# One key page group of sixteen turned by VectorE instead of TensorE, in a hybrid decoder layer

## The chip, the cores and the metric

The kernel runs on one core of a Trainium2 chip. The metric is device time in microseconds of one execution, as the median of several runs; the profile is of one execution. The engines are named as in the profile: PE (TensorE matmuls), PEld (its weight loads), DVE (VectorE), ACT (ScalarE), POOL (GpSimd) and SP (SyncE, which issues most of the transfers).

## The reference: one layer of differential attention, a gated delta rule and a conv-FFN

One decoder layer runs over a prompt of 512 tokens with 16 learned meta tokens ahead of it, and over 8 sample sequences of 8 new tokens, each with 2048 past tokens in a paged cache of 128 tokens a page. The change lies in the attention of the sample sequences:

```python
def diff_attn_sample(q, k, v, lam, k_past, v_past):
    qs = q * (d ** -0.5)
    s_past = jnp.einsum('bqhmd,bkhmd->bhmqk', qs, k_past)
    s_new = jnp.einsum('bqhmd,bkhmd->bhmqk', qs, k)
    s_new = jnp.where(jnp.tril(...), s_new, -jnp.inf)
    pr = jax.nn.softmax(jnp.concatenate([s_past, s_new], axis=-1), axis=-1)
    a = pr[:, :, 0] - lam * pr[:, :, 1]
    ...
k_past = cache_k[l][page_table].reshape(ds, -1, DA_HEADS, 2, DA_HEAD_DIM)
```

There are 4 heads with two maps of 64 channels each, so a key has 512 channels, and a page of keys is 128 x 512 floats, 256 KB. The same layer has the prompt's own differential attention (`o_a`, with an RMS norm over each head), the gated delta rule in chunks (`o_b`), one combined input projection, two sigmoid gates, an output projection and a gated FFN with a causal convolution of width 3.

## The kernel before

Everything is fp32. A product of fp32 operands is made from three products of high and low parts (`xhi`, `xlo`, `whi`, `wlo`): weights arrive as `wraw` (line 430), ACT casts the high part (line 434), DVE subtracts the low part (line 435). All matmuls are issued by `mm` (line 381) and all TensorE transposes by `transpose` (line 541).

Two generators run interleaved. `main()` does the projections, the prompt's attention head by head (`prompt_attention`) and the delta rule; `rest()` does the sample sequences' attention (`sample_attention`), the gates and branch products. `merge` counts PE work as it is issued (`self.work`) and resumes the generator that is furthest behind; a generator that has yielded a number stays away for so much PE work. The numbers come from the table `PAUSES`, by generator and index of the yield, else from the code. `Held` marks a pause that also holds while narrow work runs, and a planner then settles the order on each engine. Each engine runs its own instructions strictly in that order.

**The sample attention.** For each of four pairs of sequences (`pr`) and each of four key groups (`g`), eight pages are loaded, two pages a tile `page` (six buffers). SP issues the loads (line 1575) with an address read from the page table. Keys arrive with tokens on the partitions; the score matmul needs channels there. So PE turns each page by four transposes of 128x128 into `ps_t`, ACT or DVE copies the result to `KT` (line 1596), and 16 matmuls make the scores `ps_s<-KT,qb`. A DVE instruction (`score`, line 1427) adds the mask and takes the maximum.

**The prompt attention of one head.** For blocks of rows, the scores `ps_m` go through `score`, ACT's exponential and normalising on DVE (lines 1505 to 1512) to `S`; PE turns `S`, ACT or DVE copies it to `aT`, and `ps_t<-v,aT` and `ps_t<-vt,aT` give the output block, which ACT copies to `on` (line 1529). After the last block `head_norm` runs: four squares with sums on ACT (`hjunk`, line 1538), a multiply-add on DVE (`hss`, line 503), a power on POOL (line 504), and four scalings on DVE (`on`, line 1541). Then PE turns `on`.

The group concerned (`pr` 0, `g` 2) is issued while the first head of the prompt's attention is at its last blocks.

Of the kernel before, what the change touches and what calls it, by code (L numbers as in the profile page):

```python
# [24 lines left out]
NPG = PAST // PAGE  # L25
H = 4
# [25 lines left out]
def _lay_out_constants():  # L52
# [67 lines left out]
    for name, a in (("c0", c0), ("c1", c1), ("m0", m0), ("m1", m1)):  # L120
# [27 lines left out]
PAGES = 6  # L148
CUT_S = 832
CUT_O = 512  # L150
MAKE_W = 54.400005891
WRAW, WLO = 3, 4
LOADS_AHEAD = 5
NC = 290
# [4 lines left out]
WARM = 5  # L159
FINE = 8  # L160
MAIN_1 = 564.54
HOLD = 3.0
PAUSES = {
# [4 lines left out]
    },  # L168
# [4 lines left out]
    },  # L173
# [5 lines left out]
    },  # L179
# [4 lines left out]
    },  # L184
    "gdn_project0": {
        0: 0.24, 4: 0.94, 6: 4.89,
# [2 lines left out]
        2: 0.06, 3: 1.09, 4: 0.27, 6: 11.27,  # L189
    },  # L190
    "gdn_project2": {
        0: 0.09, 2: 0, 3: 1.19, 5: 0, 6: 9.74,
    },
# [5 lines left out]
    },  # L199
    "make0": {  # L200
        5: 1.23, 6: 0.56, 7: 0.9, 10: 0.5, 13: 0.26, 16: 0.4,
    },
    "prompt_rows0": {
        0: 6.89, 1: 1.2, 3: 7.45, 4: 0.72,
    },
    "prompt_rows1": {
        0: 2.75, 1: 0.86, 4: 1.45,
    },
    "prompt_rows2": {
        0: 7.54, 1: 1.83, 3: 7.27, 4: 1.59, 5: 0.86,  # L210
    },
    "prompt_rows3": {
        0: 7.41, 1: 1.54, 2: 0.01, 3: 2.6, 4: 0.98,
    },
    "prompt_rows4": {
        1: 1.26, 3: 3.04, 4: 2.18,
    },
    "prompt_rows5": {
        2: 0.03, 4: 0.59,
    },  # L220
    "prompt_rows6": {
        0: 7.63, 1: 1.37, 3: 1.06, 4: 1.41,
    },
    "prompt_rows7": {
        1: 1.2, 3: 2.57, 4: 1.29,
    },
# [12 lines left out]
    },  # L239
    "use0": {  # L240
        0: 0.07, 5: 1.68, 6: 0.1, 9: 0, 12: 6.56, 13: 0.11, 23: 0.6, 25: 10.39, 26: 0.26, 38: 2.47, 39: 0.1,
        51: 3.07,
    },
}
MAIN_2 = 1e9
# [11 lines left out]
class Body:  # L257
# [40 lines left out]
    def run(self):  # L298
        nc, ctx = self.nc, self.ctx
# [13 lines left out]
        with ExitStack() as sm:  # L313
            with ExitStack() as s1:
                self.opool = self.pool(s1, "opool")
                self.oa = self.t(self.opool, [128, H, NQ], "oa")
                self.ob = self.t(self.opool, [128, H, NQ], "ob")
                with ExitStack() as s2:
                    self.keep = self.pool(s2, "keep")
                    self.x = self.parts(self.pool(s2, "xpool"), "x", 8, HALF_T)  # L320
                    with ExitStack() as s:
                        first = self.embed(self.pool(s, "embed", 2, side="right"))
                    self.gproj = self.pool(s2, "gproj")
                    da = ExitStack()
                    dpool = self.pool(da, "da")
                    self.psum_m = self.pool(da, "psum_m", space=PSUM)
                    self.da_queries(dpool, first)
                    with ExitStack() as s:
                        tmp = self.pool(s, "gs", side="right")
                        self.gdn_scalars(tmp)  # L330
                        self.gdn_consts(tmp)
                    self.news = self.chain = self.spare = False

                    swo, self.wo0, self.wo_next = ExitStack(), [], 0

                    def main():
                        head = {}
                        yield from self.da_main(dpool, self.gdn_project(0, head))
                        da.close()
                        self.chain = True  # L340
                        self.psum_g = self.pool(ctx, "psum_g", space=PSUM)
                        with ExitStack() as s:
                            self.gpool = self.pool(s, "gpool")
                            yield from self.gdn(head)
                        yield from self.mix_parts(self.pool(s2, "mix"))
                        self.wo0 += self.wout_tiles(self.pool(swo, "wo0", side="right"), 0)

                    def rest():
                        with ExitStack() as s:
                            yield from self.sample_attention(self.pool(s, "sa", side="right"))  # L350
                        self.gates, self.gtpool = {}, self.pool(sm, "gates", side="right")
                        for i in range(16):
                            yield from self.gate(i)
                        while not self.spare:
                            yield None
                        yield from self.branch_a()

                    self.drain(self.merge((main(), lambda: MAIN_2 if self.chain else MAIN_1), (rest(), REST_W)))
                    self.banks = "ggsttdd"
                    self.mix()  # L360
# [1184 lines left out]
    def sample_attention(self, pool):  # L1545
        nc, a = self.nc, self.a
# [4 lines left out]
        ck = a["cache_k"][0].rearrange("n t h m d -> n t (h m d)")  # L1551
# [18 lines left out]
        def pages(cache, ids):  # L1570
# [5 lines left out]
                moves[tag] = move.ins  # L1576
            return t

        for pr in range(NB // 2):
            if pr % 2 == 0:  # L1580
                os = self.t(pool, [128, 1, 128], "oS", bufs=1)
# [1 line left out]
            mx = self.t(self.keep, [128, 5], "smx", bufs=2)  # L1583
            for g in range(4):
                sp = self.ps("s")
                kts = {}
                for u in range(2):
                    for e in range(2):
                        kp = pages(ck, [(2 * pr + e) * NPG + 4 * g + 2 * u + j for j in range(2)])
                        kt = self.t(pool, [128, H, 256], "KT", bufs=4)  # L1590
# [8 lines left out]
                for u in (1, 0):  # L1599
                    for e in (1, 0):  # L1600
                        for h in range(H):
                            self.mm(
                                sp[32 * h : 32 * h + 32, 256 * u : 256 * u + 256], self.qb[:, 2 * pr + e, h],
                                kts[u, e][:, h], start=e == 1, stop=e == 0,
                            )
                yield 0.0
# [852 lines left out]
```

## Time and profile before

| | |
|---|---|
| median of 3 runs | 1110.27 us (1109.65 to 1110.64) |
| the profiled execution | 1109.7 us, its span 1107.9 us |
| PE / DVE / ACT / POOL busy | 98% / 66% / 47% / 20% |
| page transposes on PE (line 541) | 512, 69.3 us busy |
| copies to `KT` on ACT (line 1596) | 108, 58.6 us busy |
| score matmuls `ps_s<-KT,qb` | 512 records, 34.1 us busy |

The profile gives each group of instructions as line, engine, operation, output<-input by the program's names, shape, count, busy time and mean duration. In a timeline or a chain row the first number is the start in us, the second the time. A row of a table of windows has the window, its length, then the busy time (and count) of PE, PEld, DVE, ACT and POOL, the granted clock, the share of the DMA engines, and GB/s. Matmuls overlap, so from one start to the next is less than the duration of one.

### The profile page before, as it was taken

The numbers are of one execution on the slowest core, as the hardware profiler recorded it, in microseconds if no ns is written. First come the engines' busy times: TensorE is split into PE (matmuls) and PEld (weight loads), VectorE is DVE, ScalarE is ACT, GpSimd is POOL, SyncE is SP. The second block draws the span as 40 slices with busy tenths as digits, with TensorE's granted clock in tenths as the row PEclk, the third lists the DMA queues.
The fourth block names the chain that finished last, engine by engine and source line by source line (L and its number), as shares of the span: only waits on it lengthen the run. The fifth ranks groups of instructions, "written<-read, shape, count | busy, mean of one in ns | idle before, by whom it ended". The sixth has DMA issues, their size and how long they took to land.

```text
span 1107.9 us, 23301 instructions
## 1 busy us (share of the span) xinstructions
PE 1082.5 (98%) x8554; PEld 958.0 (86%) x8554; DVE 726.1 (66%) x1891; ACT 521.2 (47%) x1258; POOL 220.4 (20%) x340
## 2 busy tenths in 40 slices
PE   8999999999999999999999999999999999999997
PEld 7888887787786787799999978999999999988886
DVE  6456667686468586465335754699999999842315
ACT  6335454465464465344333344465565555832311
POOL 4122230211101110100000004335454444200000
PEclk9999999999999999999999999999999999999999
DMA  6395325747956767722234263323233332333213
GB/s 198 78 326 164 99 72 186 255 150 250 311 189 213 237 209 229 234 69 66 72 95 135 86 180 124 115 67 107 87 98 96 96 98 77 120 111 105 90 44 124
DMA packets 167356, 156.88 MB, mean 142 GB/s; under 512 B 12307, under 2 KB 123458, under 8 KB 167241
## 3 DMA queue, kind: packets, MB, share of 16 engines
q1 hardware_dynamic: 162833, 147.00, 43.2%
q0 software_dynamic: 3008, 5.16, 1.5%
q10 hardware_dynamic: 1400, 3.22, 0.9%
q8 instruction: 68, 1.11, 0.4%
q14 instruction: 47, 0.39, 0.1%
HBM read 145.45 MB, written 9.88 MB: 140 GB/s over the span
## 4 chain that ended last, share of the span: by engine, by line
PE 80%; DVE 8%; ACT 4%; DMA 3%; issue 3%; POOL 2%; SPq 0%; DVEq 0%; ACTq 0%; POOLq 0%
PE ps_d L381 30%; PE ps_t L381 21%; PE ps_g L381 15%; PE ps_s L381 6%; PE ps_t L541 6%; ACT KT L1596 1%; PE ps_m L381 1%; DMA wraw<-in_w_out 1%; DVE wlo L435 1%; DVE cy L880 1%; DMA x<-in_x_prompt 1%; DMA page<-in_cache_v 1%; DVE xc L1217 1%; DVE row L1215 1%; DVE row L1216 1%
## 5 line engine op out<-in xcount | busy, mean ns | idle before, releaser
L435 DVE TENSOR_TENSOR wlo<-wraw,whi 128x512 fp32r<-128x512 f32 x190 | 143.2, 771 | 112.3 <-ACT whi L434 111.5
L381 PE MATMUL ps_d<-xhi,whi 128*128 128x256 f32 (+2 forms) x696 | 213.0, 309 | 0.2
L381 PE MATMUL ps_d<-xlo,whi 128*128 128x256 f32 (+2 forms) x696 | 209.6, 304 | 0.0
L381 PE MATMUL ps_d<-xhi,wlo 128*128 128x256 f32 (+2 forms) x696 | 209.1, 303 | 0.0
L434 ACT CAST whi<-wraw 128x512 fp32r<-128x512 f32 x190 | 114.0, 620 | 155.5 <-PE ps_d L381 62.2
L381 PEld LDWEIGHTS ps_d<-xlo,whi 128*128 128x128 f32 x696 | 130.7, 189 | 4.5 <-issue 4.2
L381 PEld LDWEIGHTS ps_d<-xhi,whi 128*128 128x128 f32 x696 | 130.8, 189 | 4.3 <-issue 2.6
L381 PEld LDWEIGHTS ps_d<-xhi,wlo 128*128 128x128 f32 x696 | 130.7, 189 | 1.7 <-issue 1.2
L1596 ACT COPY KT<-ps_t 128x512 f32<-128x512 f32 x108 | 58.6, 601 | 34.5 <-PE ps_t L541 28.5
L435 DVE TENSOR_TENSOR lw<-sw,hw 128x512 fp32r<-128x512 f32 x76 | 69.7, 918 | 5.2 <-ACT hw L434 5.2
L541 PE MATMUL ps_t<-consts,page 128*128 128x128 f32 x512 | 69.3, 278 | 2.5 <-DVE KT L1596 1.1
L381 PE MATMUL ps_t<-fhit,hw 128*128 128x290 f32 x228 | 67.9, 298 | 0.5 <-DVE p L2124 0.5
L381 PE MATMUL ps_t<-flot,hw 128*128 128x290 f32 x228 | 67.6, 296 | 0.0
L381 PE MATMUL ps_t<-fhit,lw 128*128 128x290 f32 x228 | 67.5, 296 | 0.0
L541 PEld LDWEIGHTS ps_t<-consts,page 128*128 128x128 f32 x512 | 56.2, 140 | 10.1 <-issue 2.7
L434 ACT CAST hw<-sw 128x512 fp32r<-128x512 f32 x76 | 46.8, 618 | 15.7 <-PE ps_g L381 10.5
L381 PEld LDWEIGHTS ps_t<-fhit,hw 128*128 128x128 f32 x228 | 43.1, 189 | 0.9 <-DVE p L2124 0.7
L2099 ACT ACTIVATE fy<-fpre,fw 128x592 f32<-128x592 f32 x22 | 19.4, 884 | 50.8 <-DVE fpre L2059 50.8
L381 PEld LDWEIGHTS ps_t<-flot,hw 128*128 128x128 f32 x228 | 43.2, 189 | 0.0
L381 PEld LDWEIGHTS ps_t<-fhit,lw 128*128 128x128 f32 x228 | 43.0, 189 | 0.0
L2101 DVE SCALAR_TENSOR_TENSOR fy<-fpre,fw,fy 128x592 f32<-128x592 f32 x44 | 36.4, 828 | 1.0 <-ACT fy L2099 0.4
L381 PE MATMUL ps_s<-KT,qb 128*32 128x256 f32 x512 | 34.1, 383 | 1.5 <-ACT KT L1596 1.2
(722 smaller groups left out, 2805.1 us busy)
## 6 DMA issues: line engine op xcount, KB each, us to landing
page<-in_cache_k SPq DMA_DIRECT2D x128, 256.0 KB, 4.5
page<-in_cache_v SPq DMA_DIRECT2D x128, 256.0 KB, 4.0
wraw<-in_w_in SPq DMA_DIRECT2D x86, 256.0 KB, 3.2
wraw<-in_w_ffn_in SPq DMA_DIRECT2D x50, 256.0 KB, 3.0
wraw<-in_w_down SPq DMA_DIRECT2D x44, 256.0 KB, 3.0
raw<-in_w_ffn_in SPq DMA_DIRECT2D x38, 256.0 KB, 2.9
wraw<-in_w_out SPq DMA_DIRECT2D x16, 256.0 KB, 3.0
x<-in_x_prompt SPq DMA_DIRECT2D x4, 512.0 KB, 7.4
```

What stands on the lines that cost most here:

```text
L381: i = self.nc.tensor.matmul(out, lhsT, rhs, **kw)
L434: self.nc.scalar.copy(hi, raw)
L435: (eng or self.nc.vector).tensor_tensor(out=lo, in0=raw, in1=hi.bitcast(F32), op=ALU.subtract)
L541: i = self.nc.tensor.transpose(out, in_, self.ident[:k, :k])
L880: nc.vector.scalar_tensor_tensor(out=y, in0=pre[:, j : j + n], scalar=self.cw[:, ch, 24 + j : 25 + j], in1=y, op0=ALU.mult, op1=ALU.add)
L1215: nc.vector.stream_shuffle(r, y, [i // BASE * BASE + j for i in range(32)])
L1216: nc.vector.tensor_tensor(out=r, in0=r, in1=lc[:, :, j : j + 1].to_broadcast([128, 5, j + 1]), op=ALU.mult)
L1217: nc.vector.tensor_tensor(out=y, in0=y, in1=r, op=ALU.subtract)
L1596: copy(kt[:, :, 128 * j : 128 * j + 128], tp)
L2099: nc.scalar.activation(y, pre[:, 0:592], AF.Identity, bias=fw[:, m, 19:20], scale=fw[:, m, 16:17])
L2101: nc.vector.scalar_tensor_tensor(out=y, in0=pre[:, j : j + 592], scalar=fw[:, m, 16 + j : 17 + j], in1=y, op0=ALU.mult, op1=ALU.add)
```

## The change

For one group of the sixteen (`TURNED`), the eight pages are loaded by 32 DMAs of 64 KB instead of 8 of 256 KB. Each moves, for one page, one 32-channel block out of every 128 channels to one quarter of the partitions, in runs of 128 bytes; the token index is split so that partition p of a quarter holds every fourth token. DVE then turns all 32x32 blocks of a tile in place, one instruction of 128x1024 for two pages, and the tile holds channels on the partitions. The 16 score matmuls read the tile itself, and write their output with strides (`keys`), so that the tokens come out in order. The 32 PE transposes and the 8 copies to `KT` (six on ACT, two on DVE) of that group are gone. Besides, `main()` waits for the end of `sample_attention` before `mix_parts`, and nearly all entries of `PAUSES` and one weight of the merge (`MAKE_W`) have new values. Lines behind the new code move by 6 and more: 541 is 547, 381 is 387, 1541 is 1547.

```diff
-MAKE_W = 54.400005891
+MAKE_W = 65.82400712811001
+L_P = 4.0
+T_P = 4.0
+TURNED = ((2,), (), (), ())
...
     "rest0": {
-        0: 0.35, 1: 1.56, 2: 0.55, 4: 0.71, 6: 0.07, 8: 1.04, 10: 1.68, 12: 1.45, 13: 1.35, 14: 1.02, 16: 4.8,
+        0: 0.35, 1: 1.56, 2: 0.55, 4: 0.71, 10: 1.66, 12: 1.45, 13: 1.35, 14: 1.02, 16: 4.8, 17: 1.03, 21: 1.11,
...
+                        while not self.sampled:
+                            yield None
                         yield from self.mix_parts(self.pool(s2, "mix"))
...
                             yield from self.sample_attention(self.pool(s, "sa", side="right"))
+                        self.sampled = True
...
+        def blocks(ids):
+
+            t = self.t(pool, [128, 2, 512], "page", bufs=PAGES)
+            for k, i in enumerate(ids):
+                tag, value = entry(ck, i)
+                page = cache_blocks[bass.ds(value, 1)]
+                for c in range(4):
+                    move = nc.sync.dma_start(
+                        t[32 * c : 32 * c + 32, k].rearrange("p (n d) -> p n d", d=32),
+                        page[:, :, :, c].rearrange("o t n d -> (o t) n d"),
+                    )
+                moves[tag] = move.ins
+            return t
+
+        cache_blocks = ck.rearrange("n (t b) e -> n t (b e)", b=4).rearrange("n t (m c d) -> n t m c d", c=4, d=32)
...
-                kts = {}
-                for u in range(2):
+                kts, keys = {}, lambda x: x
+                for u, e in [(u, e) for u in range(2) for e in range(2)] if g in TURNED[pr] else []:
+                    kts[u, e] = blocks([(2 * pr + e) * NPG + 4 * g + 2 * u + j for j in range(2)])
+                if kts:
+                    yield L_P
+                    for kp in kts.values():
+                        two = kp.rearrange("p j c -> p (j c)")
+                        nc.vector.transpose(two, two)
+                    kts = {a: kp.rearrange("p j (b h t) -> p h j b t", b=4, h=H) for a, kp in kts.items()}
+                    keys = lambda x: x.rearrange("p (j t b) -> p j b t", t=32, b=4)
+                    yield Held(T_P)
+                for u in range(0 if kts else 2):
...
-                                sp[32 * h : 32 * h + 32, 256 * u : 256 * u + 256], self.qb[:, 2 * pr + e, h],
+                                keys(sp[32 * h : 32 * h + 32, 256 * u : 256 * u + 256]), self.qb[:, 2 * pr + e, h],
```

The order on PE around the group's scores `ps_s_1363`, at the end of the first head. Before, from the last output block of the head (`ps_t_1486`) on:

```order
L381 MATMUL ps_t_1486<-v_954,aT_1478 128x128 [waits Activation_49]
L381 MATMUL ps_t_1486<-vt_358,aT_1478 128x128 [waits DVE_49]
L381 MATMUL ps_s_1363<-KT_1447,qb_356 32x256 x4
L381 MATMUL ps_s_1363<-KT_1431,qb_356 32x256 x4
L381 MATMUL ps_s_1363<-KT_1401,qb_356 32x256 x4
L381 MATMUL ps_s_1363<-KT_1376,qb_356 32x256 x4
L541 MATMUL ps_t_1533<-consts_66,page_1520 128x128 [waits DMAHW6_49,PE_49]
L541 MATMUL ps_t_1533<-consts_66,page_1520 128x128 x3
```

Now, from the same output block (`ps_t_1462`) on; `page_1364`, `page_1382`, `page_1400` and `page_1409` are the group's four tiles in the order in which DVE turns them:

```order
L387 MATMUL ps_t_1462<-v_954,aT_1454 128x128 [waits Activation_49]
L387 MATMUL ps_t_1462<-vt_358,aT_1454 128x128 [waits DVE_49]
L387 MATMUL ps_s_1363<-page_1409,qb_356 32x2x4x32 [waits DMAHW4_49,DMAHW3_49,DMAHW5_49,DMAHW2_49,DMAHW6_49,DMAHW1_49,DMAHW7_49,DMAHW0_49,DVE_49]
L387 MATMUL ps_s_1363<-page_1409,qb_356 32x2x4x32 x3
L387 MATMUL ps_s_1363<-page_1400,qb_356 32x2x4x32 x4
L387 MATMUL ps_s_1363<-page_1382,qb_356 32x2x4x32 x4
L387 MATMUL ps_s_1363<-page_1364,qb_356 32x2x4x32 x4
L547 MATMUL ps_t_1509<-consts_66,page_1496 128x128 [waits DMAHW6_49,PE_49]
```

The place of the scores is the same; they now wait for DVE, at the tile turned last. Between the head's last `ps_m` and this place stood 32 page transposes and 18 product matmuls before; none stands there now. On DVE before, at the same place (`S_736` is the score instruction of the group, `hss` and `on` belong to head_norm):

```order
L1523 COPY aT_1478<-ps_t_1482 16x128
L503 TENSOR_SCALAR hss_1490<-hss_1490 128x4
L1427 ISA S_736,smx_737<-ps_s_1363,consts_66 128x512
L1427 ISA smx_737 128x1
L1541 SCALAR_TENSOR_TENSOR on_1098<-on_1098,hss_1490,sub_562 128x128 x4
L1596 COPY KT_1532<-ps_t_1533 128x4x128
```

and now (the turn of `page_1364` stands 37 instructions ahead of this `hss`):

```order
L1529 COPY aT_1454<-ps_t_1458 16x128 [waits PE_49,Pool_49]
L509 TENSOR_SCALAR hss_1466<-hss_1466 128x4 [waits Activation_49]
L1547 SCALAR_TENSOR_TENSOR on_1098<-on_1098,hss_1466,sub_562 128x128 [waits Pool_49]
L1614 STREAM_TRANSPOSE page_1382<-page_1382 128x1024 [waits DMAHW4_49,DMAHW5_49,DMAHW3_49,DMAHW6_49,DMAHW2_49,DMAHW7_49,DMAHW1_49,DMAHW0_49]
L1547 SCALAR_TENSOR_TENSOR on_1098<-on_1098,hss_1466,sub_562 128x128 x3
L1614 STREAM_TRANSPOSE page_1400<-page_1400 128x1024 [waits DMAHW4_49,DMAHW5_49,DMAHW3_49,DMAHW6_49,DMAHW2_49,DMAHW7_49,DMAHW1_49,DMAHW0_49]
L1614 STREAM_TRANSPOSE page_1409<-page_1409 128x1024 [waits DMAHW4_49,DMAHW5_49,DMAHW3_49,DMAHW6_49,DMAHW2_49,DMAHW7_49,DMAHW1_49,DMAHW0_49]
L1433 ISA S_736,smx_737<-ps_s_1363,consts_66 128x512 [waits PE_49]
```

Three turns stand behind `hss` and the first `on`, and the score instruction, which stood between `hss` and `on`, has moved behind the turns. On SP, the group's 32 loads stand where its 8 stood; the loads of the next two tiles and of the weights (`wraw`) follow them as before.

More of the change, by code (lines that the diff above doesn't have):

```diff
@@ L191 @@
     "gdn_project2": {
-        0: 0.09, 2: 0, 3: 1.19, 5: 0, 6: 9.74,
+        0: 0.02, 2: 0, 3: 0.54, 5: 0, 6: 9.74,
     },
     "main0": {
[4 rows of a table removed]
[4 rows of a table added]
     },
     "make0": {
-        5: 1.23, 6: 0.56, 7: 0.9, 10: 0.5, 13: 0.26, 16: 0.4,
+        1: 0.36, 4: 0.16, 5: 2.42, 6: 0.6, 7: 0.9, 10: 0.5, 13: 0.26, 16: 0.4,
     },
     "prompt_rows0": {
-        0: 6.89, 1: 1.2, 3: 7.45, 4: 0.72,
+        0: 2.06, 1: 1.2, 3: 7.45, 4: 0.46,
     },
     "prompt_rows1": {
-        0: 2.75, 1: 0.86, 4: 1.45,
+        0: 2.75, 1: 0.86, 3: 4.52, 4: 1.45,
     },
     "prompt_rows2": {
-        0: 7.54, 1: 1.83, 3: 7.27, 4: 1.59, 5: 0.86,
+        0: 7.54, 1: 1.83, 3: 7.43, 4: 1.86, 5: 0.86,
     },
     "prompt_rows3": {
-        0: 7.41, 1: 1.54, 2: 0.01, 3: 2.6, 4: 0.98,
+        0: 6.65, 1: 0.92, 2: 0.01, 3: 2.6, 4: 0.28,
     },
     "prompt_rows4": {
-        1: 1.26, 3: 3.04, 4: 2.18,
+        1: 0.67, 3: 3.04, 4: 2.17,
     },
     "prompt_rows5": {
-        2: 0.03, 4: 0.59,
+        1: 0.75, 2: 0.01, 4: 0.59,
     },
     "prompt_rows6": {
-        0: 7.63, 1: 1.37, 3: 1.06, 4: 1.41,
+        0: 7.72, 1: 1.37, 3: 1.06, 4: 1.41,
     },
     "prompt_rows7": {
-        1: 1.2, 3: 2.57, 4: 1.29,
+        1: 1.2, 3: 2.5, 4: 1.29,
     },
     "rest0": {
[11 rows of a table removed]
[11 rows of a table added]
     },
     "use0": {
-        0: 0.07, 5: 1.68, 6: 0.1, 9: 0, 12: 6.56, 13: 0.11, 23: 0.6, 25: 10.39, 26: 0.26, 38: 2.47, 39: 0.1,
-        51: 3.07,
+        0: 0.05, 5: 1.16, 6: 0.1, 9: 0, 12: 5.34, 13: 0.11, 19: 0, 23: 0.24, 25: 13.34, 26: 0.26, 27: 0.54,
+        38: 2.47, 39: 0.1, 51: 3.07,
     },
@@ L331, in run @@
                         self.gdn_consts(tmp)
-                    self.news = self.chain = self.spare = False
+                    self.news = self.chain = self.spare = self.sampled = False
                     swo, self.wo0, self.wo_next = ExitStack(), [], 0
```

52 rows, old and new, of the table PAUSES are left out of this document.

## The prediction

> **What bounds the kernel now.** I read the page's busy shares first, then PE by stage, then the chain of waits around the place where the turned group will stand.
>
> ```profile
> span 1107.9 us, 23301 instructions
> PE 1082.5 (98%) x8554; PEld 958.0 (86%) x8554; DVE 726.1 (66%) x1891; ACT 521.2 (47%) x1258; POOL 220.4 (20%) x340
> L541 PE MATMUL ps_t<-consts,page 128*128 128x128 f32 x512 | 69.3, 278 | 2.5 <-DVE KT L1596 1.1
> 60.00:112.00 52.00, 51.42 (x442) 43.04 (x440) 32.85 (x108) 24.53 (x62) 13.20 (x25) 1.00 0.75 250
> 112.00:560.00 448.00, 434.66 (x4213) 363.66 (x4213) 290.08 (x1013) 223.68 (x630) 55.43 (x106) 1.00 0.57 176
> ```
>
> PE is busy for 98% of the span, and the time is in first order PE's work plus the gaps in it. So whatever leaves PE is gained in full, and whatever makes PE wait is lost in full, DVE's, ACT's and the DMA's own work counting only where PE stands behind it. From 60 to 112 us, where the turned group lies, PE is idle for 0.58 us; from 112 to 560 us for 448 − 434.66 = 13.3 us.
>
> **What is taken from PE.** 32 of the 512 page transposes go.
>
> ```profile
> 95.17 0.45 PE ps_m L381 x4
> ...
> 99.34 0.24 PE ps_d L381 x2
> 99.58 1.55 PE ps_t L541 x14
> ...
> 103.60 0.69 PE ps_t L381 x4
> 104.28 0.02 issue
> 104.31 0.28 ACT on L1529
> ...
> 104.61 0.41 ACT hjunk L1538 x2
> ...
> 106.60 1.06 POOL hss L504
> ...
> 107.69 1.14 DVE on L1541 x4
> ```
>
> These are pieces of the chain of waits. Fourteen transposes take 1.55 us of it, 0.111 us each, so 32 give **−3.5 us**. The eight copies to KT that leave ACT and DVE hide behind PE today; what they free is counted at nothing. The 16 score matmuls stay. Their output is now strided in PSUM; no row has that form, so it costs between 0 and once more their present time (1.93 us, the 104.20 row below). I take 0, because it is the same number of elements from the same kind of matmul.
>
> **What PE waits for now.** In the order of PE, the head's last two matmuls with aT (ps_t<-v,aT and ps_t<-vt,aT) are followed directly by the turned scores, and the first of these reads the page that VectorE turns last. On VectorE the last three turns stand behind head_norm: after hss and the first `on`. head_norm itself starts from those same two matmuls. In the chain above, the matmuls end at 104.28 us; ACT's copy, four squares with their sums, DVE's hss and POOL's power come next, and the first `on` starts at 107.69, 3.41 us later. Before, PE had score matmuls, page transposes and products to do in that time:
>
> ```profile
> 103.89 0.39 PE L381 MATMUL ps_t<-vt,aT 128*128 128x128 f32 x2
> 104.20 1.93 PE L381 MATMUL ps_s<-KT,qb 128*32 128x256 f32 x32
> 106.07 1.53 PE L541 MATMUL ps_t<-consts,page 128*128 128x128 f32 x12
> 109.48 2.10 PE L541 MATMUL ps_t<-consts,page 128*128 128x128 f32 x16 [0.52 <-DVE KT L1596]
> L1225 DVE STREAM_TRANSPOSE cc<-row x4: 338/346/346, 265.4 to 508.4; 128x160 f32<-128x160 f32 x4
> L1261 DVE STREAM_TRANSPOSE row<-cc x4: 306/311/313, 268.9 to 513.6; 128x128 f32<-128x128 f32 x4
> ```
>
> After, it has nothing: everything later in its order stands behind the scores. Their release needs 3.41 us, four `on` (1.14 us) and three turns of 128x1024. The two nearest rows give 311 ns at 128 columns and 346 at 160, 1.09 ns a column, so 1024 columns take 311 + 896 x 1.09 = 1.29 us, or 1.25 us from one to the next with some overlap. The gap is 3.41 + 1.14 + 3 x 1.25 = **+8.3 us**. If a turn went at half the time a column the gap would be 6.4, if at twice 12.0. I take the slope, since both rows are the same instruction on the same type. The first turn stands 37 instructions ahead of hss and adds 1.2 us to a VectorE that is 63% busy (32.85 of 52 us): nothing.
>
> **What the lost filler uncovers.** The 32 page transposes and 18 product matmuls that stood between the head's last ps_m (ends 95.62) and its last ps_t<-vt,aT (ends 104.28) also covered the softmax between them. Without them, PE has 104.28 − 95.62 − 3.55 − 2.1 = 3.0 us to do there (18 products at 0.12, from the pair at 99.34). The chain that it waits for is on VectorE and ACT:
>
> ```profile
> 97.01 0.34 DVE L1427 CUSTOM_DVE_ANT_0 S<-ps_m,consts,mx 128x128 f32<-128x128 f32 x1
> 98.41 0.67 DVE L1389 COPY v<-ps_t 128x512 f32<-128x512 f32 x1
> 99.23 0.41 ACT L1503 ACTIVATE S<-S,nm 128x144 f32<-128x144 f32 x1 [0.61 <-DVE nm L1501]
> 102.31 0.37 DVE L1512 SCALAR_TENSOR_TENSOR S<-S,rc,S 128x144 f32<-128x144 f32 x1
> 103.34 0.28 DVE L1523 COPY aT<-ps_t 16x128 f32<-16x128 f32 x1 [0.66 <-PE ps_t L541]
> ```
>
> Two maps' scores and maxima come to about 1.4 us (the 128-wide one 0.34, its neighbours 0.1 to 0.2), the copies of v and vt that stand between them 0.9, the exponential with its sum 0.6, normalising 0.8, then PE's two transposes 0.4, the copy 0.28 and the last matmuls 0.66: 5.0 us against 3.0. Exposed: **+1.9 us** (0.5 if VectorE's copies of v come earlier, 2.5 at most). VectorE's copies of KT stood in this chain too and go, which I have left out of the sum of 5.0 already. The stall of 0.52 us at 109.48, on a copy of VectorE's, is overtaken by the longer one: **−0.5**.
>
> **PE after a long gap.** The span's first matmuls are the only ones that follow a long idle time; the last two rows are PE's longest single waits from 112 to 560 us (total, times, longest).
>
> ```profile
> 1.10 2.50 PE L381 MATMUL ps_s<-warm 128*128 128x128 f32 x10 [1.10 <-DVE warm L556]
> 3.39 2.59 PE L381 MATMUL lnb<-row,one 128*128 128x512 f32 x4
> 5.82 0.38 PE L381 MATMUL ps_s<-warm 128*128 128x128 f32 x2
> PE ps_s L381 <- DMA page<-in_cache_v: 1.7, 2, 1.3
> PE ps_t L541 <- DVE on L1541: 1.2, 1, 1.2
> ```
>
> The same matmul takes 0.21 to 0.23 us from start to start at 1.1 us ((2.50 − 0.42) / 9, where 0.42 is one alone) and 0.11 at 5.8 us (0.38 − 0.27). So PE runs at half pace there for between 2.3 and 4.7 us, though the clock column reads 1.00 from the first slice on. No single wait of those is longer than 1.3 us, so whether 8 us bring the slow start back isn't seen. If they do, PE loses half of 2.3 to 4.7 us, 1.2 to 2.4. I take **+1.5**, because part of it falls on page transposes that wait for their copies anyway; if they don't, 0.
>
> [...]
>
> **The transfers.** Eight loads of 256 KB become 32 of 64 KB in runs of 128 bytes.
>
> ```profile
> 66.26 10.00 SPq L1575 DMA_DIRECT2D page<-in_cache_k  x12
> 76.55 15.06 SPq L430 DMA_DIRECT2D wraw<-in_w_in  x4
> L1575 SPq DMA_DIRECT2D page<-in_cache_k x128: 332/333/1207, 55.3 to 417.6; - x128
> q1 hardware_dynamic: 1492, 0.12, 19.4%
> 80.00:88.00 8.00, 7.94 (x57) 7.29 (x58) 5.61 (x23) 3.23 (x9) 1.76 (x5) 1.00 0.29 76
> ```
>
> SP spends 0.33 us on one issue and, with the queues full of 256-KB loads, 10.00 / 12 = 0.83 us from one to the next, so 32 take 11 to 27 us from 66.26. On the 16 DMA engines, the queue row (of the window from 16 to 24 us: 1492 packets of 80 bytes on average) gives 0.194 x 8 us x 16 / 1492 = 17 ns a packet; 16384 packets make 17 us. From 80 us on the engines are 71% free. I expect the last to land at about 90 us; the last three turns run from 108. So this is hidden: each load would have to take (107.7 − 66.3) / 32 = 1.29 us before the last turn were late. Behind the 32 on SP stand four loads of wraw and the next pages. With 24 issues more ahead of them, at 0.33 to 0.83, wraw leaves 8 to 20 us later than 76.55; its products stand behind the turned scores, after 112, so it is hidden too, with less room.
>
> **The rest.** The table of pauses is retuned throughout and moves products from this stage to later ones. The wait for the sample attention before mix_parts costs nothing (the last keys are loaded at 417.6 us, the row of L1575, and the delta rule, which main has to end first, still turns blocks at 508.4 us, the row of L1225). I take 0 for the retuning, between −6 and +2: the gain can come from the 13.3 us of idle PE alone.
>
> **Sum**: −3.5 + 8.3 + 1.9 − 0.5 + 1.5 = +7.7 on the profiled execution's 1109.7 us, 1117.4. The median of the runs is 0.57 above that execution, so **1118.0 us**.
>
> **Rivals.**
> 1. *The gap stays, the slow start doesn't come*: 1116.5. For it: the clock column never leaves 1.00. Against: the first matmuls.
> 2. *Faster: the slack is given back.* In the gap ACT, VectorE and the queues run ahead, and the later waits of PE (13.3 us in 112 to 560) shrink. Against rival 1's 1116.5 it decides from 6.2 us given back on, and with 8.5 the time is 1108.0. For it: the waits are on ACT, VectorE and loads, all of which could be early. Against: the next head's own head_norm, the last row of the fence on the long gap, is a chain that starts from PE itself, so a head start doesn't shorten it. Between 4 and 8 us given back the time is within 0.2% of before.
> 3. *The runs of 128 bytes land late*: at 1.6 us a load the last lands at 66.3 + 51 = 117.5 us, 10 us after the turn wants it: 1128. For it: nothing here moves 128-byte runs in bulk. Against: 17 ns a packet.
> [...]
> 4. *A turn takes twice the slope*: +3.7, 1121.7.
>
> **How the numbers follow.** Forecast 0.48 (1114.5 to 1121), rival 1 0.18, rival 4 0.07, rival 3 0.07, slack given back enough to be faster 0.12, 4 to 8 us of it 0.08. About 0.2%, 2.2 us, can be told from no change. Slower: 0.48 + 0.18 + 0.07 + 0.07 = 0.80. The range leaves out rival 3 and the faster case: 1110 to 1123, from half the slack given back to a slow turn with the slow start at its dearest.
>
> **What would show it.** Right: in the timeline of PE after ps_t<-vt,aT a gap of 7 to 9 us that ends on VectorE's last turn; turns of 1.2 to 1.3 us, three of them after hss; 480 page transposes; matmuls after the gap at 0.2 us. Wrong: PE waits less than 4 us before the turned scores; or the wait ends on a DMA; or PE's idle time from 112 to 560 us falls below 8 us.

## The result, and the profile after

The changed kernel takes 1118.28 us (median of 3 runs, 1117.71 to 1120.26) against 1110.27 before: 1.0077 times as long, 95% interval 1.0054 to 1.0100. The profiled execution took 1117.71 us, 8.0 more than that of before.

The head of the page of the changed kernel, PE and its clock in 40 slices, and from the table of windows the three stages around the group's scores:

```profile
span 1115.9 us, 23310 instructions
PE 1078.3 (97%) x8522; PEld 954.2 (86%) x8522; DVE 730.0 (65%) x1893; ACT 517.9 (46%) x1252; POOL 222.3 (20%) x340
PE   9986999999999999999999999999999999999997
...
PEclk9998999999999999999999999999999999999999
60.00:112.00 52.00, 39.15 (x327) 32.08 (x329) 29.62 (x98) 18.00 (x49) 12.63 (x25) 0.92 0.62 160
112.00:560.00 448.00, 433.90 (x4235) 362.18 (x4228) 290.03 (x1007) 222.32 (x624) 53.70 (x104) 1.00 0.59 185
103.00:111.00 8.00, 0.00 (x0) 0.00 (x0) 4.81 (x8) 1.79 (x9) 1.05 (x1) 0.56 0.00 1
111.00:114.40 3.40, 3.39 (x33) 1.39 (x33) 0.00 (x0) 0.00 (x0) 0.00 (x0) 0.54 0.35 109
114.40:118.00 3.60, 3.60 (x29) 2.65 (x26) 2.69 (x5) 2.48 (x5) 0.00 (x0) 1.00 0.79 261
```

PE has less work, and a slice (84 to 112 us) in which it is busy for six tenths only. From 60 to 112 us it was idle for 0.58 us before and is idle for 12.85 now; from 112 to 560 us for 13.3 before and 14.1 now. From 103 to 111 us it does nothing at all, and for the 3.4 us after that its granted clock is 0.54.

The timelines of PE and VectorE there (start, time, and in brackets the idle time before it and what ended it):

```profile
98.90 0.33 PE L547 MATMUL ps_t<-consts,S 128*128 128x128 f32 x1 [0.52 <-ACT aT L1525]
99.06 0.61 PE L387 MATMUL ps_t<-v,aT 128*128 128x128 f32 x4
100.06 0.49 PE L387 MATMUL ps_t<-vt,aT 128*128 128x128 f32 x2 [0.39 <-DVE aT L1529]
101.41 0.44 PE L547 MATMUL ps_t<-consts,S 128*128 128x128 f32 x2 [0.86 <-DVE S L1518]
102.17 0.49 PE L387 MATMUL ps_t<-v,aT 128*128 128x128 f32 x2 [0.32 <-ACT aT L1525]
102.50 0.39 PE L387 MATMUL ps_t<-vt,aT 128*128 128x128 f32 x2
111.01 3.46 PE L387 MATMUL ps_s<-page,qb 128*32 128x256 f32 x32 [8.12 <-DVE page L1614]
114.39 2.16 PE L547 MATMUL ps_t<-consts,page 128*128 128x128 f32 x16
```

```profile
104.95 0.17 DVE L509 TENSOR_SCALAR hss<-hss 128x4 f32<-128x4 f32 x1 [2.71 <-ACT hjunk L1544]
106.29 0.35 DVE L1547 SCALAR_TENSOR_TENSOR on<-on,hss,sub 128x128 f32<-128x128 f32 x1 [1.17 <-POOL hss L510]
106.67 1.25 DVE L1614 STREAM_TRANSPOSE page<-page 128x1024 f32<-128x1024 f32 x1
107.83 0.83 DVE L1547 SCALAR_TENSOR_TENSOR on<-on,hss,sub 128x128 f32<-128x128 f32 x3
108.58 2.37 DVE L1614 STREAM_TRANSPOSE page<-page 128x1024 f32<-128x1024 f32 x2
```

The chain is the one that the order showed: PE ends the head's last matmuls at 102.9, ACT, VectorE and POOL run head_norm, the first `on` starts at 106.3, three turns follow among the other `on`, and PE goes on when the last is done. On SP an issue takes 0.563 us where one of 256 KB took 0.333. From one load to the next it is 26.72 / 32 = 0.83 us, as between the larger loads before, but there are 32 loads now:

```profile
66.44 26.72 SPq L1592 DMA_DIRECT2D page<-in_cache_k  x32
93.78 2.34 SPq L1581 DMA_DIRECT2D page<-in_cache_k  x4
96.23 0.94 SPq L436 DMA_DIRECT2D wraw<-in_w_in  x2
L1592 SPq DMA_DIRECT2D page<-in_cache_k x32: 563/564/1352, 66.4 to 92.6; - x32
```

### The profile page after: what moved, and what is told of

It is laid out like the page before. It is cut to its first block, busy times and chain, and to the rows that moved or that the text cites. A ratio compares the mean times of both kernels' runs of the same rounds, so it can differ in the third digit from the quotient of the medians.

```text
span 1115.9 us, 23310 instructions
## 1 busy us (share of the span) xinstructions
PE 1078.3 (97%) x8522; PEld 954.2 (86%) x8522; DVE 730.0 (65%) x1893; ACT 517.9 (46%) x1252; POOL 222.3 (20%) x340
## 4 chain that ended last, share of the span: by engine, by line
PE 75%; DVE 10%; ACT 5%; DMA 5%; issue 3%; POOL 1%; SPq 1%; DVEq 0%; ACTq 0%; POOLq 0%
PE ps_d L387 28%; PE ps_t L387 20%; PE ps_g L387 14%; PE ps_t L547 6%; PE ps_s L387 6%; DMA page<-in_cache_v 2%; DMA wraw<-in_w_out 1%; DVE wlo L441 1%; ACT KT L1627 1%; DMA wraw<-in_w_ffn_in 1%; PE ps_m L387 1%; DVE S L1433 1%; DVE cy L886 1%; DMA x<-in_x_prompt 1%; ACT whi L440 1%
## 5 line engine op out<-in xcount | busy, mean ns | idle before, releaser
L1627 ACT COPY KT<-ps_t 128x512 f32<-128x512 f32 x102 | 55.2, 603 | 43.5 <-PE ps_t L547 37.6
L547 PE MATMUL ps_t<-consts,page 128*128 128x128 f32 x480 | 64.8, 278 | 2.8 <-DMA page<-in_cache_k 1.5
L547 PEld LDWEIGHTS ps_t<-consts,page 128*128 128x128 f32 x480 | 53.0, 140 | 10.5 <-issue 2.7
L387 PE MATMUL ps_s<-page,pT 128*32 128x256 f32 x512 | 33.0, 383 | 3.2 <-DMA page<-in_cache_v 3.2
```

Source lines behind the costliest of these rows:

```text
L387: i = self.nc.tensor.matmul(out, lhsT, rhs, **kw)
L547: i = self.nc.tensor.transpose(out, in_, self.ident[:k, :k])
L1627: copy(kt[:, :, 128 * j : 128 * j + 128], tp)
```

## The experiments

The theory was that PE waits for turns which stand behind head_norm. The rivals were the loads in short runs, the retuned table and the strided scores. Each kernel is timed beside runs of the kernel before (medians 1110.0 to 1110.4 us), so the ratio to it is given, with its 95% interval; for the changed kernel it is 1.0077 (1.0054 to 1.0100).

**e2: the turns ahead of head_norm.** VectorE's `hss` is queued behind the last turn; PE's order stays.

```diff
-                        nc.vector.transpose(two, two)
+                        self.turned = nc.vector.transpose(two, two).ins
...
-        self.rsqrt(ss, ss, 1.0 / 128, EPS, rows, nh)
+        with ExitStack() as s:
+            if getattr(self, "turned", None) is not None:
+                s.enter_context(self.tc.issue_after(self.turned))
+                self.turned = None
+            self.rsqrt(ss, ss, 1.0 / 128, EPS, rows, nh)
```

> The changed kernel, with VectorE's hss put behind the last turn, so that three turns run ahead of head_norm instead of behind it; PE's order is the same. Theory: the turns start when aT is copied, 0.6 us before the head's last matmuls end, and take 3.7 us, so the gap falls from 8.1 to about 3.1 us; the time is 1111.8 with full pace after the gap, 1113.3 if 3.1 us still slow PE down. Rival (the loads are late, or the strided scores cost the time): the gap stays near 8 us and the time at 1118.

1114.66 us, 1.0034 (1.0019 to 1.0050). From its timelines and its windows:

```profile
102.16 3.50 DVE L1618 STREAM_TRANSPOSE page<-page 128x1024 f32<-128x1024 f32 x3
105.71 3.55 PE L387 MATMUL ps_s<-page,qb 128*32 128x256 f32 x32 [2.69 <-DVE hss L509]
102.00:103.00 1.00, 1.00 (x4) 0.72 (x4) 0.89 (x2) 0.00 (x0) 0.00 (x0) 0.61 0.81 270
```

The gap is 2.7 us instead of 8.1, and the scores begin 5.3 us earlier. The row puts the wait down to `hss`, which stands right behind the last turn; that turn ends at 105.66. So the place of the turns is what PE waited for. The scores are still slow. The clock reads 0.61 from 102 to 103 us and 0.50 after, so it fell at about 102.2 (0.2 us at 1.00 and 0.8 at 0.50 give 0.6), while PE was at work and before the gap of 2.7 us began. The median is 1.4 us above the expectation, and 3.6 below that of the changed kernel. Its profiled execution, the slowest of its runs, is only 0.6 us faster than the changed kernel's: it waits 6.5 us for pages of values later on, where the changed kernel waits 3.2.

**e5: no turns at all.** The four turns are left out, so the group's scores aren't those of the keys.

```diff
-                        two = kp.rearrange("p j c -> p (j c)")
-                        nc.vector.transpose(two, two)
+                        pass
```

> The changed kernel without its four turns on VectorE (the scores of that group read the pages as loaded, so they aren't scores of the keys); the 32 loads stay. PE's order is the same: scores right behind the head's last matmuls. Theory (the gap waits for turns behind head_norm): the loads have landed by 96 us, so the gap of 8.1 us and the slow start after it go; PE then meets head_norm's `on` a little early, about 0.5 us. Time 1118.3 - 8.1 - 1.5 + 0.5 = 1109.2, 1107.5 to 1110.5. Rival (32 loads of 128-byte runs hold PE up): 1114 or more, with PE waiting on a DMA.

1113.1 us, 1.0030 (1.0012 to 1.0048); its profiled execution took 1110.67. Its timeline of PE:

```profile
102.39 1.93 PE L387 MATMUL ps_s<-page,qb 128*32 128x256 f32 x32
104.25 1.53 PE L547 MATMUL ps_t<-consts,page 128*128 128x128 f32 x12
108.28 0.66 PE L547 MATMUL ps_t<-consts,page 128*128 128x128 f32 x4 [2.49 <-DVE KT L1626]
```

The gap and the slow scores are gone though all 32 loads stay, so neither the loads nor the strided output hold PE there. The expectation (1107.5 to 1110.5) was too low, since the next wait was not 0.5 us: VectorE's copy of the next page stands behind `on` and PE waits 2.5 us for it. Against the changed kernel's profiled execution the sum is −8.1 − 1.5 + 2.5 = −7.1, and 1110.67 − 1117.71 = −7.04. But that pair is the fastest run of each kernel. Between the medians the gain is 5.2 us; the runs of e5 spread from 1110.67 to 1119.96, and what sets them apart was not settled.

**e11: PE kept busy in the gap.** 42 matmuls on constants go ahead of the scores, which overwrite their result. They show as 84 records: 60 in the gap, 24 in the softmax ahead of it.

```diff
+                if g in TURNED[pr]:
+                    for k in range(42):
+                        nc.tensor.matmul(sp[:, :128], self.ident, self.ident, start=True, stop=True)
```

> The changed kernel with 42 more matmuls of 128x128 on constants, whose result the group's scores overwrite; 30 of them stand between the head's last matmuls and the turned scores, 12 in the softmax chain ahead. At 0.22 us each they fill 6.6 us. The planner also moves the second turn ahead of the first `on`, beside POOL's power, so the last turn ends about 1.1 us earlier. Theory (PE's pace falls in the gap): with PE kept busy the scores take 1.93 us instead of 3.46 and the time is 1118.3 - 1.5 - 1.1 = 1115.7. Rival (the scores are slow for another reason, their stride or the tile): 3.4 us again, and 1117.2.

1117.32 us, 1.0078 (1.0055 to 1.0102). Its timeline of PE and its windows:

```profile
102.12 6.86 PE L1632 MATMUL ps_s<-consts 128*128 128x128 f32 x60
109.33 1.93 PE L387 MATMUL ps_s<-page,qb 128*32 128x256 f32 x32 [0.35 <-DVE page L1614]
103.00:111.00 8.00, 7.65 (x86) 6.73 (x84) 4.72 (x8) 1.23 (x7) 1.05 (x1) 1.00 0.01 3
```

With PE busy the clock stays at 1.00 and the same scores take 1.93 us. The slow start is the clock's, worth 3.46 − 1.93 = 1.5 us there, and the stride costs nothing. The scores are the theory's, but the total is the rival's 1117.2: the ratio shows no gain over the changed kernel, where 2.6 us were expected. The scores end 3.2 us earlier (at 111.26 instead of 114.47); 4.9 us of waiting for pages of values against 3.2 take 1.7 of it back, and where the rest goes was not settled.

**e3 and e4: the table and the group apart.** e3 has the new table and no group turned, e4 the turned group with the old table.

```diff
-TURNED = ((2,), (), (), ())
+TURNED = ((), (), (), ())
```

> The changed kernel with no group turned (TURNED empty): the new table of pauses and merge weight alone. Theory: the retuning is worth nothing by itself, 1110.3 within 2 us. Rival (the retuned table, made for other work, loses the 8 us): 1115 or more. If it gains, up to 6 us, the turned group costs that much more than the 8 us that were measured.

> The changed kernel with the table of pauses and the merge weight of before: the turned group alone. The planner again puts the scores right behind the head's last matmuls and three turns behind hss. Theory: the same gap of 8 us with the slow start, 1117 to 1120. Rival (the loss is the retuning's): 1107 to 1111.

e3: 1110.01 us, 0.9996 (0.9983 to 1.0008). e4: 1120.52 us, 1.0115 (1.0079 to 1.0151), and PE waits at the same place as in the changed kernel:

```profile
PE ps_s L387 <- DVE page L1614: 8.1, 1, 8.1
```

The retuning by itself is worth nothing that can be measured, and the group alone brings the whole loss. Whether the table wins some of it back (1.0077 with it, 1.0115 without) can't be told: the intervals overlap.

**e6: eight loads, four turns.** The pages are loaded as before and turned all the same; the blocks are then not whole keys.

```diff
-                for c in range(4):
-                    move = nc.sync.dma_start(
-                        t[32 * c : 32 * c + 32, k].rearrange("p (n d) -> p n d", d=32),
-                        page[:, :, :, c].rearrange("o t n d -> (o t) n d"),
-                    )
+                move = nc.sync.dma_start(t[:, k], ck[bass.ds(value, 1)].rearrange("o t e -> (o t) e"))
```

> The changed kernel with the eight loads of before (256 KB, runs of 2 KB, tokens on the partitions; the turned blocks are then not whole keys), and the four turns kept. The planner, which has the pages earlier, puts all turns far ahead of hss and leaves products between the head's last ps_m and the scores. Theory (turning on VectorE itself is hidden, the loss comes from the order that late loads bring): 3.5 us below before, 1106.8, 1105.5 to 1108.5, and no gap above 1 us there. Rival (the turns cost PE their time wherever they stand): 1111 or more.

1108.86 us, 0.9979 (0.9962 to 0.9996): below before, as the theory had it, though the median lies just outside the range (1105.5 to 1108.5) and 1.4 us of the 3.5 are seen. Its profile shows 4.7 us of waiting for pages of values, where the kernel before waits 1.7. The turns (first and last start in the row) and the scores:

```profile
L1610 DVE STREAM_TRANSPOSE page<-page x4: 1234/1236/1240, 79.2 to 86.7; 128x1024 f32<-128x1024 f32 x4
103.82 1.93 PE L387 MATMUL ps_s<-page,qb 128*32 128x256 f32 x32
```

All turns are done at 88 us, and products stand on PE between the head's last softmax and the scores. So turning on VectorE is hidden here, and the planner's order around it follows the loads: with 32 of them ahead of the weights on SP, it put three turns behind `hss` and no product in front of the scores. In e1, e9 and e10 below, which leave 8 or 16 on SP, all turns stand ahead of `hss` too. Why the planner decides so is argued from these orders, not shown.

**e1: one load a page.** The same runs of 128 bytes by one transfer of 128 partitions a page.

```diff
-                for c in range(4):
-                    move = nc.sync.dma_start(
-                        t[32 * c : 32 * c + 32, k].rearrange("p (n d) -> p n d", d=32),
-                        page[:, :, :, c].rearrange("o t n d -> (o t) n d"),
-                    )
+                move = nc.sync.dma_start(
+                    t[:, k].rearrange("p (n d) -> p n d", d=32),
+                    page.rearrange("o t n c d -> (o c) t n d"),
+                )
```

> One DMA a page (128x512, still in runs of 128 bytes) instead of four of 32 partitions; nothing else in the code changes, but the planner now puts all four turns ahead of hss and leaves 18 products between the head's last ps_m and the scores. Theory (the loss is VectorE's turns standing behind head_norm, and PE without filler): the gap of 8.1 us ahead of the turned scores falls under 0.5 us, the scores run at full pace (1.9 us instead of 3.5), the time is 1106.5 to 1109, below before. Rival (16384 packets of 128 bytes are what costs): the time stays above 1115, and PE waits on a DMA.

1133.44 us, 1.0199 (1.0168 to 1.0230). Its SP rows, a window while they run, and the last turn on VectorE:

```profile
66.40 37.64 SPq L1591 DMA_DIRECT2D page<-in_cache_k  x8
L1591 SPq DMA_DIRECT2D page<-in_cache_k x8: 716/4604/7692, 66.4 to 99.4; - x8
88.00:96.00 8.00, 2.25 (x12) 2.04 (x11) 2.79 (x6) 0.48 (x1) 0.00 (x0) 0.82 0.34 54
110.98 1.25 DVE L1613 STREAM_TRANSPOSE page<-page 128x1024 f32<-128x1024 f32 x1 [8.49 <-DMA page<-in_cache_k]
```

The theory's expectation fell, and the time is the rival's. The scores ran at full pace (1.93 us) without a gap ahead of them, but the loads move 54 GB/s and SP is held for 38 us; VectorE waits 16.1 us for them, with the softmax behind its turns, so the wait for a load is on VectorE and PE waits for VectorE. Why the rate is so low isn't shown: the DMA share of the window is 0.34, and no run shows which engines were used.

**e9 and e10: half of the loads on another engine's queue.** Blocks 1 and 2 of each page are issued by ACT, or by POOL.

```diff
-                    move = nc.sync.dma_start(
+                    move = (nc.scalar if c in (1, 2) else nc.sync).dma_start(
```

> The changed kernel with two of each page's four loads issued by ACT instead of SP. The planner now puts all four turns ahead of hss: two early, two between the head's last softmax and its aT copy. Theory (the loss comes from the order that 27 us of issues on SP bring): the gap of 8.1 us falls to 2.5 us or less, the copy of aT comes up to 2.4 us later, and ACT, which issues 16 loads of about 0.6 us among its copies, gives back some of it: 1110 to 1114. Rival (ACT's issues wait for the lanes of loads that SP issued, and hold its copies up): 1116 or more, with PE waiting on copies of ACT.

> The same with two of each page's four loads issued by POOL, which is idle for 80%. All four turns again stand ahead of hss. Theory: as with ACT, but without its copies in the way: the gap falls below 2 us, 1109 to 1113. Rival (POOL's own way of issuing makes 512 runs a load slow, and its power and memsets for the head stand behind them): PE waits for POOL's work or for these loads, 1116 or more.

e9: 1114.88 us, 1.0048 (1.0025 to 1.0070). e10: 1114.04 us, 1.0043 (1.0019 to 1.0067). Both lie about 1 us above what was expected; 4.5 and 3.6 us are lost instead of 8, and both are still behind before. PE and ACT in e9, then VectorE and PE in e10:

```profile
102.02 1.22 PE L387 MATMUL ps_t<-v,aT 128*128 128x128 f32 x4 [5.48 <-ACT aT L1525]
L1592 ACTq DMA_DIRECT2D page<-in_cache_k x16: 571/580/813, 72.3 to 100.9; - x16
100.63 1.25 DVE L1614 STREAM_TRANSPOSE page<-page 128x1024 f32<-128x1024 f32 x1 [0.96 <-DMA page<-in_cache_k]
102.91 0.35 PE L547 MATMUL ps_t<-consts,S 128*128 128x128 f32 x1 [3.05 <-DVE S L1518]
```

The gap at the scores is gone, and another has opened ahead of the head's matmuls: in e9 ACT issues loads until 100.9 us and copies `aT` behind them, and PE waits 5.5 us for it where the theory had that copy come 2.4 us later at most. That is the rival's wait, at less than its price; that ACT's issues waited for SP's loads isn't shown (the two waits of ACT's queue on the line of the loads took 38 ns at most). In e10, whose profiled execution was the slowest of its runs (1121.73), a turn waits for a load and VectorE's `S` stands behind that turn. An issue takes POOL 0.652 us there, and SP 0.570 (medians). The scores are slow in both (3.31 and 3.64 us).

**e7 and e8: the group elsewhere.** The first, or the second, group of the second pair of sequences is turned instead.

```diff
-TURNED = ((2,), (), (), ())
+TURNED = ((), (0,), (), ())
```

> The changed kernel with another group turned: the first of the second pair of sequences, far from any head_norm, its scores behind a dozen products on PE. Theory: with work on PE between the turns and the scores there is no gap of 8 us; the saving of 3.5 us shows in part, 1106.8 to 1109.5. Rival (32 loads at 0.83 us each hold SP for 27 us wherever they stand, and other loads come late): 1111 or more, with PE waiting on DMAs behind the group.

> As the run before, with the second group of the second pair: its turns stand singly among the delta rule's short instructions on VectorE, the last one at the end of a long chain there. Theory: a gap again where the last turn stands behind a chain, but a shorter one than 8 us; 1108 to 1113. Rival: the place doesn't matter and the time is that of the run before within 1 us.

e7: 1142.87 us, 1.0301 (1.0277 to 1.0324). e8: 1161.59 us, 1.0452 (1.0435 to 1.0470). Neither was expected. In e8 the last turn stands behind a chain of the delta rule (its row of waits):

```profile
PE ps_s L387 <- DVE page L1614: 20.8, 1, 20.8
```

That is the theory's mechanism at more than twice its size, and it is 20.8 of 51 us lost; the rest was not taken apart. In e7 no wait on a turn is left. SP issues the 32 loads in 25.5 us there too, and PE is busy for 80.5 of the 100 us from 200 on, in the changed kernel for 96.4; the longest of its waits is 5.6 us on a `kn` of VectorE. The time fits e7's rival, but its sign is missing: from 195 to 320 us PE waits for no transfer. Which part of the new order is late, and whether the loads brought it, was not settled; the table of pauses is tuned for the other place.

## Why the prediction was right

By its own steps, with what each measured:

| term | predicted | measured |
|---|---|---|
| 32 transposes off PE | −3.5 | 480 left of 512; their busy time 69.3 to 64.8, −4.5 |
| the gap ahead of the scores | +8.3 | 8.12 |
| softmax uncovered | +1.9 | 0.52 + 0.39 + 0.86 + 0.32 = 2.09 |
| the stall on a copy of VectorE | −0.5 | gone from that place |
| PE after the gap | +1.5 | 3.46 − 1.93 = 1.53 |
| retuning | 0 | 0.9996 (0.9983 to 1.0008) |
| waits and work that the sum has not | 0 | +2.5 − 1.2, see below |
| sum | +7.7 | +8.0 |

- The gap came step by step as predicted. From the head's last matmul (102.89 us) to the first `on` (106.29) it is 3.40 us, against 3.41; the four `on` take 0.35 + 0.83, against 1.14; the three turns 1.25 + 2.37 = 3.62, against 3.75. The slope from two short turns held: 1.24 us for 128x1024 by the row of e6, where 1.29 was worked out. Rival 4 is out. Three turns, not one, were on the path, because the order had put them there.
- The softmax came out by its steps too. The prediction's own figures give 5.04 − 3.01 = 2.0 and not 1.9; the four waits come to 2.09.
- The slow start came, with the right size for a wrong reason. The prediction read the clock column as 1.00 everywhere and went by the first matmuls; after the gap the column shows it too, 0.54 for the 3.4 us from 111.0. It took 1.5 because part of the slow time would fall on page transposes that wait anyway; all of it fell on the scores. e11 shows that it is the clock, by keeping PE busy, and rival 1, that the slow start stays away, is out. By the clock column full pace is back 3.1 us after the scores begin (0.50 from 113 to 114 us, 0.86 from 114.0 to 114.5), 3.3 in e2 (0.50 from 108 to 109 us, 0.98 from 109 to 110) and an estimated 4.3 in e4 (0.57 from 110 to 114 us, as a mean of 0.50 and 1.00). The clock reads 0.95 from 103 to 104 us and 0.50 after that, so it fell 1 us behind PE's last matmul. In e2 and e4 it fell before their gaps began. That the gap brought the slow start is therefore not shown (rows under the hardware below).
- The loads are mis-sized on SP and right in their effect. An issue takes 0.563 us with 512 runs, not 0.333, so the 32 take 26.7 us, the upper end of 11 to 27, and the weights leave 20 us later, the end of 8 to 20. The 0.83 us from one load to the next came again with loads of a quarter of the size, so it isn't shown to come from queues full of large loads. The last turn waited for no load: a load of 64 KB in 128-byte runs landed in 2.8 us (median), where one of 256 KB landed in 4.5 before. Rival 3 is out for this order; in e1, e9 and e10 turns did wait for loads.
- Something the prediction did not say: it took the order as given and the loads as hidden. e6 and e1 show that the order itself follows the loads. With eight quick loads the same turns cost nothing.
- Slack was not given back. PE's idle time from 112 to 560 us went from 13.3 to 14.1 us, so rival 2 is out too.
- The sum is closer than its parts, and that is luck. Between the two profiled executions PE's busy time fell by 4.2 us although the slow scores added 1.5, so 5.7 us of work left it and not 3.5: 4.5 by the row of page transposes (0.135 us each, where the chain gave 0.111), and 1.2 elsewhere. Its idle time rose by 12.2 us, from 25.4 (1107.9 − 1082.5) to 37.6 (1115.9 − 1078.3), and only 8.12 + 2.09 − 0.52 = 9.7 of that are the prediction's. Of the other 2.5, 1.66 is a wait for VectorE's maxima at 79.7 us, ahead of the group. e3 has it as well, the kernel before and e4 have not, so the new table brought it. The 2.2 us too much and the 2.5 too little cancel.

```profile
L547 PE MATMUL ps_t<-consts,page 128*128 128x128 f32 x480 | 64.8, 278 | 2.8 <-DMA page<-in_cache_k 1.5
79.71 0.49 PE L387 MATMUL ps_m<-kT,oa 64*128 64x128 f32 x4 [1.66 <-DVE mx L1433]
```

- One wait has grown, and no term stands for it: PE waits 1.7 us for pages of values in the kernel before and 1.4 in e3, and 3.1 to 6.5 us in the changed kernel and in all ten other runs, e5 without turns and e6 with its eight quick loads among them. Why was not settled.

## What to carry to other kernels

Work moved from the bounding engine to an idler one was free here where the bounding engine had other work queued ahead of what needs it (e6, no gap), and cost 8.12 us of waiting where it had none (the changed kernel): look in the order at what stands ahead of the moved work on its new engine, and at what the bounding engine has to do until then. A slower way of loading can hurt without any wait on a transfer (8.12 us here, with no turn that waited for a load), by what the planner puts late and by the work that is no longer there to fill a gap. When a gap of several us is priced, add the slow pace that followed it here, 1.5 us.

## What the runs showed of the hardware

- PE's clock fell twice with no long gap ahead. In e2 it read 0.61 from 102 to 103 us, with PE at work and the gap of 2.7 us still ahead; in e4 it read 0.87 from 99 to 100 us, 1 us before its gap. Ahead of the fall in e2 PE was about half busy for four us (1.92 of them from 98 to 102). The like of it brought no fall in e5: PE was busy for 1.96 us of the same four, and the clock stayed at 1.00, also through a gap of 2.5 us behind two us of full work. What brings the fall is not settled by these runs. The rows are of e2, of e4 and of the changed kernel (one each), and of e5.

```profile
98.00:100.00 2.00, 1.10 (x8) 0.72 (x7) 1.64 (x8) 1.24 (x5) 0.96 (x2) 1.00 0.81 238
100.00:101.00 1.00, 0.36 (x2) 0.16 (x2) 0.82 (x4) 0.31 (x2) 1.00 (x3) 1.00 0.79 259
101.00:102.00 1.00, 0.46 (x3) 0.23 (x3) 0.40 (x2) 0.27 (x1) 0.63 (x2) 1.00 0.73 122
```

```profile
99.00:100.00 1.00, 0.68 (x3) 0.44 (x4) 0.28 (x1) 0.27 (x1) 0.39 (x2) 0.87 0.84 305
103.00:104.00 1.00, 0.00 (x0) 0.00 (x0) 0.00 (x0) 0.94 (x5) 0.00 (x0) 0.95 0.03 11
```

```profile
98.00:100.00 2.00, 1.14 (x7) 0.88 (x7) 1.57 (x8) 1.28 (x5) 1.19 (x2) 1.00 0.93 297
100.00:101.00 1.00, 0.14 (x3) 0.01 (x1) 0.83 (x4) 0.27 (x1) 1.00 (x3) 1.00 0.98 223
101.00:102.00 1.00, 0.68 (x4) 0.44 (x5) 0.28 (x1) 0.27 (x1) 0.40 (x2) 1.00 1.04 345
102.00:104.00 2.00, 2.00 (x36) 1.20 (x35) 0.00 (x0) 1.41 (x7) 0.00 (x0) 1.00 0.27 94
106.00:108.00 2.00, 0.00 (x0) 0.00 (x0) 2.00 (x7) 0.00 (x0) 0.00 (x0) 1.00 0.95 304
```

- The time that SP spends on one issue was longer with more runs in it: 0.333 us for 128 runs of 2 KB, 0.563 for 512 of 128 bytes, and 0.716 to 7.7 (median 4.6) for the 2048 of e1. What SP does in the longest of these isn't shown.
- The shape of a transfer mattered beside its runs: a page of 256 KB in the same 128-byte runs took 4 x 0.83 = 3.3 us of SP's time in four transfers, and 37.64 / 8 = 4.7 us in one.
